# An encoder layer on one core: the mixer's key block ahead of its values, and the values as 2x2 blocks with seven products in three pairs

## The chip, the core and the metric

One Trainium2 chip, of which the kernel uses one core. The metric is the device time of one execution in microseconds (us). A core has TensorE for matrix products (PE in the profile, its weight loads PEld), VectorE (DVE), ScalarE (ACT), GpSimd (POOL) and the queues that issue transfers, SyncE's (SP) above all.

## The reference

One layer on 256 tokens of 2048 values in float32: a gated feed-forward network, a mixer, and a second feed-forward network, each with a norm in front and behind.

```python
ff = swiglu(rms_norm(x, pre_norm_ffn1[layer]), w_ffn1_gate_up[layer], w_ffn1_down[layer])
x = x + 0.5 * rms_norm(ff, post_norm_ffn1[layer])
h = rms_norm(x, pre_norm_mix[layer])
q_h, i_h, f_fwd, f_bwd, g_h, q_a, k_a, v_a = jnp.split(h @ w_mix_in[layer], split_at, axis=-1)
y_h = hgrn2_mixer(q_h, i_h, f_fwd, f_bwd, g_h, ...)
y_a = window_attention(q_a, k_a, v_a, ...)
mixed = jnp.concatenate([y_h, y_a], axis=-1) @ w_mix_out[layer]
x = x + rms_norm(mixed, post_norm_mix[layer])
...
```

The change is in `h @ w_mix_in`, a product of 256x2048 with 2048x6656. Its columns 1024 to 2047 are `i_h`, the **values** of the recurrence; columns 6144 to 6655 are keys and values of the attention, called the **key block** here. The other columns are projected in pairs of heads later.

## The kernel before, in words

**Precision.** Every operand of a large product is taken apart into a high part of reduced precision (a cast on ScalarE, L177) and the low rest (a subtraction on VectorE, L178). A product is then three matmuls: high by high, high by low, low by high. A weight tile of 128x2048 (`raw`, three buffers, 1 MB) is taken apart in two halves of 128x1024, named `h` and `l`, with five buffers each. The tokens lie transposed in `xt`, as high and low parts of 16 chunks of 128 input values; in a chunk stand 256 tokens, two halves `m` of 128.

**The norm.** `xt` holds the tokens times the gain, without the norm's factor. The factor of each token (`rs2`) comes from the squares of the residual X (`square_x`, L255, on ScalarE, one quarter of 512 values at a time), a sum and a scale on VectorE (L183, L185), a power on GpSimd (L187) and a copy (L264). It is applied to the products afterwards: where tokens lie along partitions by a scale of ScalarE, where they lie along columns by the matrix `R`. `spread` (L284) makes `R`: two multiplications of a unit matrix, a matmul by ones (L291) and a copy out of the accumulators (L292).

**Four blocks with seven products.** Class `Blocks` computes a 256x1024 result as 2x2 blocks, input values two chunks (a *pair*, 256 values) at a time. A plain pair takes 8 block products of 3 matmuls (24), a mixed pair seven (21), at the price of sums of the token blocks (`sums_of`, L406) and of the weight blocks (`seven`, L476, with the additions L486, L490 and L492 on VectorE), and of a `fold` at the end (L526) that adds four product banks into the four sums. There are eight accumulator banks in all, four named `pa` and four `pb`. Sums of token blocks of very different size would lose precision; so the second half of the tokens is first multiplied by a power of two, the **ratio** of the two halves' factors (`even`, L1073), and the norm's factor is replaced by `rest` (`power_and_rest`, L266). Before the change the two feed-forward networks and the output projection use these blocks, and the mixer's input projection uses none.

**The start of the mixer.** The stage before (`finish`, L736) ends with a list whose order on TensorE, VectorE and ScalarE is that of the source (`manual_schedule`, L828): updates of X, transposes of X into `xt` (L211, L228, L233), and between them the products of chunks 0 to 7 with the first 512 value columns (`LeadN`, L345), in two banks named `vbanks`. Behind it nothing has a fixed order, and the scheduler sets it by when it takes things to be ready:

```python
for cg in range(2):
    sl = [pa(), pa()] if cg else vbanks
    if cg == 0:
        pre_stats()
        ...
    proj_N(w_in, 1024 + cg * 512, 512, xt, sl, k0=0 if cg else 8)
    for m in range(2):
        nc.scalar.mul(vh[:, m, cg * 512 : (cg + 1) * 512], sl[m], rs2[:, m : m + 1])
```

The matmuls of `proj_N` are L375 to L377 (`products_N`). Then comes the key block, also by `proj_N_pieces` with `spread()` at its piece 16, and then four head pairs by `headpair` (L1597; matmuls L322 and L327).

Of the kernel before, what the change touches and what calls it, by code (L numbers as in the profile page):

```python
# [11 lines left out]
F32 = mybir.dt.float32  # L12
F32R = mybir.dt.float32r
# [24 lines left out]
def hymba_layer_kernel(  # L38
# [37 lines left out]
    def nm(s):  # L76
        uid[0] += 1
        return f"{s}_{uid[0]}"

    def pa():  # L80
        return psum.tile([P, 512], F32, tag="pa", name=nm("pa"))
# [94 lines left out]
    def split_act(hi, lo, src):  # L176
        nc.scalar.copy(hi, src)  # L177
        nc.vector.tensor_tensor(lo, src, hi.bitcast(F32), ALU.subtract)  # L178
# [62 lines left out]
    def pre_stats():  # L241
        with tc.issue_after(last["act"].ins):
            pre_stats_now()
# [37 lines left out]
        nc.vector.tensor_scalar(rest[:, 1:2], rest[:, 1:2], two[:, 0:1], None, ALU.mult)  # L281
        nc.vector.tensor_copy(rest[:, 0:1], rs2[:, 0:1])

    def spread(factor=rs2, n=2):  # L284

        ps = pb()
        for m in range(n):
            nc.vector.tensor_scalar(
                R[:, m * P : (m + 1) * P], ident, factor[:, m : m + 1], None, ALU.mult
            )  # L290
        nc.tensor.matmul(ps[:, : n * P], ones, R[:, : n * P], start=True, stop=True)  # L291
        nc.vector.tensor_copy(R[:, : n * P], ps[:, : n * P])  # L292


    def xcol(xt, k, part=None):
# [83 lines left out]
    def proj_N(*a, **kw):  # L379
        for _ in proj_N_pieces(*a, **kw):  # L380
            pass

    def proj_N_pieces(w, c0, n, xt, slot, k0=0):

        kn = 2048 // n
        half = kn // 2
        for kc in range(k0 // kn, KT // kn):
            hs, ls = split_load(source_N(w, c0, n, kc))
            for m in range(2):
                for kk in range(kn):  # L390
                    i = kk // half
                    products_N(xt, slot, m, kc * kn + kk, hs[i], ls[i], kk % half * n, n)
                    yield
# [215 lines left out]
    class Pairs(Blocks):  # L609
# [26 lines left out]
        def source(self, u):  # L636
            return Pairs.part(self.w, u, self.now)
# [267 lines left out]
    def pair_of(xt, u):  # L905
        return xt[u // 4][:, u % 4 * 2 : u % 4 * 2 + 2]

    class Gated(Blocks):


# [127 lines left out]
    def ffn(gated, w_dn, post_gain, again, gain=None, lead=None, aside=None):  # L1038

        with ExitStack() as st:  # L1040
# [31 lines left out]

            def even(u):  # L1073

                x = gated.tiles[u].rearrange("p k i t -> p (k i) t")[:, :, P:T]
                nc.vector.tensor_tensor(
                    x, x.bitcast(F32), R[:, None, 0:P].to_broadcast([P, 4, P]), ALU.mult
                )

            def sums_in(u):  # L1080
                x = gated.tiles[u].bitcast(F32)
# [428 lines left out]
    def again_from(src):  # L1510
# [4 lines left out]

        return again

    vbanks = [pa(), pa()]
    xt = ffn(
        gated,  # L1520
        w_ffn1_down[0],
        post_norm_ffn1,
        again_from(x[0]),
        gain=lambda: later["cols"][:, 0:16],
        lead=LeadN(w_mix_in[0], 1024, vbanks),
        aside=other_vectors,
    )
    cols = later["cols"]
# [3 lines left out]
    with ExitStack() as s2:  # L1532
# [21 lines left out]
        def lower_bounds():  # L1554
            l0, l1 = cols[:, 32:48], cols[:, 48:64]
            nc.vector.tensor_tensor(lbm, l0, l1, ALU.max)
            nc.vector.tensor_tensor(e0, l0, lbm, ALU.subtract)
            nc.vector.tensor_tensor(e1, l1, lbm, ALU.subtract)
            nc.scalar.activation(e0, e0, AF.Exp)
            nc.scalar.activation(e1, e1, AF.Exp)  # L1560
            nc.vector.tensor_tensor(e1, e0, e1, ALU.add)
            nc.vector.reciprocal(e1, e1)
            nc.vector.tensor_tensor(lb, e0, e1, ALU.mult)
            nc.vector.tensor_scalar(oml, lb, -1.0, 1.0, ALU.mult, ALU.add)

        w_in = w_mix_in[0]
        vh = mid.tile([P, 2, 1024], F32, tag="vh", name="vh")
        for cg in range(2):
            sl = [pa(), pa()] if cg else vbanks
            if cg == 0:  # L1570
                pre_stats()
                with tc.issue_after(last["rs2"].ins):
                    lower_bounds()
            proj_N(w_in, 1024 + cg * 512, 512, xt, sl, k0=0 if cg else 8)
            for m in range(2):
                nc.scalar.mul(
                    vh[:, m, cg * 512 : (cg + 1) * 512], sl[m], rs2[:, m : m + 1]
                )

# [34 lines left out]
            return z  # L1616


        sl = [pa(), pa()]
        for i, _ in enumerate(proj_N_pieces(w_in, 6144, 512, xt, sl)):  # L1620
            if i == 16:
                spread()
        va = mid.tile([P, 2, 256], F32, tag="va", name="va")
        kz = mid.tile([P, 2, 256], F32, tag="q", name="kz")
        for m in range(2):
            nc.scalar.mul(kz[:, m, :], sl[m][:, :256], rs2[:, m : m + 1])
            nc.scalar.mul(va[:, m, :], sl[m][:, 256:], rs2[:, m : m + 1])
        kT = mid.tile([P, 2, T], F32, tag="kT", name="kT")

        def turned_keys():  # L1630
# [129 lines left out]
        def gates(half):  # L1760

            sl = [pa(), pa()]
            for _ in proj_N_pieces(w_in, 4096 + half * 512, 512, xt, sl):
                side_step()
            g = mid.tile([P, 2, 512], F32, tag="g", name=nm("g"))
            for m in range(2):
                by = rs2[:, m : m + 1]
                nc.scalar.activation(g[:, m, :], sl[m], AF.Sigmoid, scale=by)
                nc.vector.scalar_tensor_tensor(g[:, m, :], sl[m], by, g[:, m, :], ALU.mult, ALU.mult)
            return g  # L1770
# [246 lines left out]
```

## Time and profile before

| what | value |
|---|---|
| time, median of 3 runs | 1823.05 us (1822.35 to 1823.59) |
| the profiled execution | 1824.3 us |
| its span, first to last instruction | 1822.5 us |
| mean granted clock of TensorE | 0.999 |
| busy: PE, DVE, ACT | 99%, 88%, 62% of the span |

The profile is one execution. A row of a timeline gives start and duration in us, engine, line, operation, output and inputs, shapes and a count; in square brackets stands the idle time of that engine before it and what ended it. A row of a group gives the count, the busy time and the mean duration of one in ns. A window row gives its length, each engine's busy time with a count, the granted clock of TensorE, the share of the transfer engines and GB/s. The chain of waits followed back from the end gives the start and length of each piece.

### The profile page before, as it was taken

To read this page: it belongs to the slowest core of one execution; us is meant where nothing else is said; L and a number is where in the kernel's file an instruction comes from. 1 tells how busy PE (TensorE), PEld (TensorE's weight loads), DVE (VectorE), ACT (ScalarE), POOL (GpSimd) and SP (SyncE) were. 2 spreads that over 40 slices of the span, in tenths; PEclk is the share of its full clock that TensorE was granted. 3 is DMA by queue.
4 is the path that set the end of the run, shared out by engine and by line. 5 is a ranking of instruction groups with operands and counts; after the bars stand their busy time and mean duration, and the time that the engine had idled before them with its cause. 6 is when DMAs were issued, how large, how long until landed. Compare 5 with 4: busy or idle time off the path is not lost.

```text
span 1822.5 us, 23466 instructions
## 1 busy us (share of the span) xinstructions
PE 1808.9 (99%) x8420; PEld 1502.0 (82%) x8420; DVE 1605.0 (88%) x2073; ACT 1137.1 (62%) x1508; POOL 162.9 (9%) x155
## 2 busy tenths in 40 slices
PE   9999999999999999999999999999999999999998
PEld 7888888888888888888888888888888888888886
DVE  7999999999989989477687798899999999998986
ACT  7565666666666657476587556556666666566653
POOL 1011111111011100000000000111111111011110
PEclk9999999999999999999999999999999999999999
DMA  8889999998698995655454456889999999699894
GB/s 303 240 235 284 278 281 257 250 261 247 224 343 263 300 300 191 196 183 176 162 174 150 162 208 243 253 242 266 283 271 269 256 248 252 195 339 302 274 303 160
DMA packets 212052, 447.59 MB, mean 246 GB/s; under 512 B 11752, under 2 KB 46656, under 8 KB 211168
## 3 DMA queue, kind: packets, MB, share of 16 engines
q1 hardware_dynamic: 180032, 385.14, 60.7%
q0 software_dynamic: 31904, 60.96, 19.5%
q8 instruction: 66, 1.08, 0.2%
q14 instruction: 50, 0.41, 0.1%
HBM read 433.46 MB, written 12.60 MB: 245 GB/s over the span
## 4 chain that ended last, share of the span: by engine, by line
PE 86%; DVE 7%; ACT 3%; DMA 2%; issue 2%; POOL 0%; DVEq 0%; ACTq 0%; SPq 0%; POOLq 0%
PE pa L454 37%; PE pb L454 32%; PE pa L322 5%; DVE l L178 4%; PE pa L327 3%; PE pa L377 2%; PE pa L375 2%; PE pa L376 2%; DMA raw<-in_w_ffn_down_dram 2%; ACT h L177 1%; PE pa L1131 1%; PE pb L1131 1%; DMA raw<-in_w_ffn_gate_up_dram 0%; DVE la L178 0%; PE pb L1738 0%
## 5 line engine op out<-in xcount | busy, mean ns | idle before, releaser
L177 ACT CAST h<-raw 128x1024 fp32r<-128x1024 f32 (+1 forms) x867 | 854.8, 1013 | 465.3 <-PE pb L454 152.9
L178 DVE TENSOR_TENSOR l<-raw,h 128x1024 fp32r<-128x1024 f32 (+1 forms) x867 | 987.8, 1170 | 134.4 <-ACT h L177 100.6
L454 PE MATMUL pa<-h,xt 128*128 128x512 f32 x1096 | 384.9, 392 | 0.1
L454 PE MATMUL pb<-h,xt 128*128 128x512 f32 x940 | 336.7, 392 | 0.3 <-DVE pb L1188 0.3
L454 PEld LDWEIGHTS pa<-h,xt 128*128 128x128 f32 x1096 | 206.0, 188 | 44.2 <-DVE xt L233 0.6
L454 PE MATMUL pa<-l,xt 128*128 128x512 f32 x548 | 214.0, 391 | 0.0
L454 PEld LDWEIGHTS pb<-h,xt 128*128 128x128 f32 x940 | 176.5, 188 | 42.5 <-DVE pb L1195 3.6
L454 PE MATMUL pb<-l,xt 128*128 128x512 f32 x470 | 183.3, 390 | 0.0
L967 POOL DMA_DIRECT2D raw<-in_w_ffn_gate_up_dram x78 | 94.6, 1212 | 733.8 <-DVE l L178 665.8
L454 PE MATMUL pb<-h,ht 128*128 128x512 f32 x452 | 159.2, 389 | 0.0
L454 PE MATMUL pa<-h,ht 128*128 128x512 f32 x452 | 159.1, 389 | 0.0
L322 PE MATMUL pa<-xt,h 128*128 128x512 f32 x512 | 124.5, 393 | 0.2 <-ACT h L177 0.2
L454 PEld LDWEIGHTS pa<-l,xt 128*128 128x128 f32 x548 | 103.2, 188 | 20.6 <-DVE l L178 0.8
L454 PE MATMUL pa<-h,xs 128*128 128x512 f32 x312 | 111.6, 389 | 0.0
L322 PEld LDWEIGHTS pa<-xt,h 128*128 128x128 f32 x512 | 93.8, 188 | 18.7 <-ACT h L177 0.6
L454 PE MATMUL pb<-h,xs 128*128 128x512 f32 x312 | 108.7, 389 | 0.0
L454 PEld LDWEIGHTS pb<-l,xt 128*128 128x128 f32 x470 | 88.3, 188 | 16.8
L454 PEld LDWEIGHTS pb<-h,ht 128*128 128x128 f32 x452 | 84.8, 188 | 17.6
L454 PEld LDWEIGHTS pa<-h,ht 128*128 128x128 f32 x452 | 84.9, 188 | 17.5
L454 PE MATMUL pa<-l,ht 128*128 128x512 f32 x226 | 88.2, 390 | 0.9 <-DVE l L178 0.9
L454 PE MATMUL pb<-l,ht 128*128 128x512 f32 x226 | 87.9, 389 | 0.0
L1273 POOL DMA_DIRECT2D raw<-in_w_ffn_down_dram x38 | 46.0, 1212 | 374.2 <-DVE la L178 337.2
(292 smaller groups left out, 2575.6 us busy)
## 6 DMA issues: line engine op xcount, KB each, us to landing
raw<-in_w_ffn_gate_up_dram SPq DMA_DIRECT2D x350, 512.0 KB, 5.9
raw<-in_w_ffn_down_dram SPq DMA_DIRECT2D x88, 1024.0 KB, 7.8
raw<-in_w_mix_in_dram SPq DMA_DIRECT2D x52, 1024.0 KB, 5.0
raw<-in_w_ffn_gate_up_dram POOLq DMA_DIRECT2D x78, 512.0 KB, 8.1
raw<-in_w_ffn_down_dram POOLq DMA_DIRECT2D x38, 512.0 KB, 10.1
raw<-in_w_mix_out_dram SPq DMA_DIRECT2D x16, 1024.0 KB, 5.0
ht<-away SPq DMA_DIRECT2D x24, 512.0 KB, 10.3
away<-ht SPq DMA_DIRECT2D x16, 512.0 KB, 7.0
```

Source lines behind the costliest of these rows:

```text
L177: nc.scalar.copy(hi, src)
L178: nc.vector.tensor_tensor(lo, src, hi.bitcast(F32), ALU.subtract)
L322: nc.tensor.matmul(slot[f], weights(hs, kk, f), xcol(xt, k), start=(k == 0), stop=(k == KT - 1))
L327: nc.tensor.matmul(slot[f][:, 0:T], weights(ls, kk, f), xcol(xt, kh * 8 + kk, 0), start=False, stop=False,)
L375: nc.tensor.matmul(dst, xh, h[:, o : o + n], start=(k == 0), stop=False)
L376: nc.tensor.matmul(dst, xh, l[:, o : o + n], start=False, stop=False)
L377: nc.tensor.matmul(dst, xl, h[:, o : o + n], start=False, stop=(k == KT - 1))
L454: nc.tensor.matmul(self.bank(at), lhs, rhs, start=(n == 1), stop=n in (ends, self.of[at]), skip_group_check=n > ends,)
L967: nc.gpsimd.dma_start(raw[:, 0:1024].rearrange("p (k c) -> p k c", k=2), self.source(u, g)[:, :, 1], accum_op=ALU.add,)
L1131: nc.tensor.transpose(bank[:, o : o + P], zs[m][:, k * P : (k + 1) * P], ident)
L1273: nc.gpsimd.dma_start(raws[i][:, 0:1024].rearrange("p (k c) -> p k c", k=2), Pairs.part(w_dn, u, r)[:, :, 512:1024], accum_op=ALU.add,)
```

## The change

The stage before now leads in chunks 0 to 7 of the key block in place of the first value columns. The whole rest of the key block and of the values stands in a block whose order on TensorE, VectorE and ScalarE is that of the source. In it the squares of the last quarters, the power and the ratio come first, around the key block's products; then the second half of the tokens is multiplied by the ratio, pair by pair, as soon as the key block has read it. The values are then one set of 2x2 blocks over 1024 columns, in the order of pairs 0 to 7, with pairs 3, 5 and 6 mixed. Since the tokens now carry the ratio, `R` and the gates use `rest` in place of `rs2`. The diff:

```diff
--- before.py
+++ after.py
@@ -281,7 +281,7 @@
         nc.vector.tensor_scalar(rest[:, 1:2], rest[:, 1:2], two[:, 0:1], None, ALU.mult)
         nc.vector.tensor_copy(rest[:, 0:1], rs2[:, 0:1])
 
-    def spread(factor=rs2, n=2):
+    def spread_begin(factor, n=2):
 
         ps = pb()
         for m in range(n):
@@ -289,7 +289,11 @@
                 R[:, m * P : (m + 1) * P], ident, factor[:, m : m + 1], None, ALU.mult
             )
         nc.tensor.matmul(ps[:, : n * P], ones, R[:, : n * P], start=True, stop=True)
-        nc.vector.tensor_copy(R[:, : n * P], ps[:, : n * P])
+        return ps[:, : n * P]
+
+    def spread(factor=rs2, n=2):
+
+        nc.vector.tensor_copy(R[:, : n * P], spread_begin(factor, n))
 
 
     def xcol(xt, k, part=None):
@@ -905,6 +909,13 @@
     def pair_of(xt, u):
         return xt[u // 4][:, u % 4 * 2 : u % 4 * 2 + 2]
 
+    def even_half(x):
+
+        x = x.rearrange("p k i t -> p (k i) t")[:, :, P:T]
+        nc.vector.tensor_tensor(
+            x, x.bitcast(F32), R[:, None, 0:P].to_broadcast([P, 4, P]), ALU.mult
+        )
+
     class Gated(Blocks):
 
 
@@ -1072,10 +1083,7 @@
 
             def even(u):
 
-                x = gated.tiles[u].rearrange("p k i t -> p (k i) t")[:, :, P:T]
-                nc.vector.tensor_tensor(
-                    x, x.bitcast(F32), R[:, None, 0:P].to_broadcast([P, 4, P]), ALU.mult
-                )
+                even_half(gated.tiles[u])
 
             def sums_in(u):
                 x = gated.tiles[u].bitcast(F32)
@@ -1515,14 +1523,14 @@
 
         return again
 
-    vbanks = [pa(), pa()]
+    kvbanks = [pa(), pa()]
     xt = ffn(
         gated,
         w_ffn1_down[0],
         post_norm_ffn1,
         again_from(x[0]),
         gain=lambda: later["cols"][:, 0:16],
-        lead=LeadN(w_mix_in[0], 1024, vbanks),
+        lead=LeadN(w_mix_in[0], 6144, kvbanks),
         aside=other_vectors,
     )
     cols = later["cols"]
@@ -1565,17 +1573,97 @@
 
         w_in = w_mix_in[0]
         vh = mid.tile([P, 2, 1024], F32, tag="vh", name="vh")
-        for cg in range(2):
-            sl = [pa(), pa()] if cg else vbanks
-            if cg == 0:
-                pre_stats()
-                with tc.issue_after(last["rs2"].ins):
-                    lower_bounds()
-            proj_N(w_in, 1024 + cg * 512, 512, xt, sl, k0=0 if cg else 8)
+
+        class Values(Blocks):
+
+
+            def source(self, u):
+                return Pairs.part(w_in, u, 1)
+
+            def left_sums(self, u):
+                return self.sums[u]
+
+            def folded(self):
+                return [
+                    [y[:, n, :] for n in range(2)]
+                    for y in (
+                        keepy.tile([P, 2, 512], F32, tag=f"yt{4 + m}", name=nm("y"), bufs=1)
+                        for m in range(2)
+                    )
+                ]
+
+        def value_sums(u):
+
+            z, s = (keepy.tile([P, 4, P], F32, tag=f"sy{i}", name=nm("vs"), bufs=1) for i in range(2))
+            x = pair_of(xt, u).bitcast(F32)
+            whole = z.rearrange("p j t -> p (j t)").rearrange("p (k t) -> p k t", k=2)
+            nc.vector.tensor_tensor(whole, x[:, :, 0, :], x[:, :, 1, :], ALU.add)
+            w = keepy.tile([P, 4, 2, P], F32R, tag=f"yt{VALUES.index(u)}", name=nm("xs"), bufs=1)
+            split_act(w[:, :, 0, :], w[:, :, 1, :], sums_of(whole, s))
+            values.sums[u] = w
+
+        VALUES = (3, 5, 6)
+        values = Values({u: pair_of(xt, u) for u in range(KT // 2)}, dict.fromkeys(VALUES))
+        va = mid.tile([P, 2, 256], F32, tag="va", name="va")
+        kz = mid.tile([P, 2, 256], F32, tag="q", name="kz")
+        ordered = {mybir.EngineType.PE, mybir.EngineType.DVE, mybir.EngineType.Activation}
+        with tc.manual_schedule(engines=ordered):
+            late = [load(source_N(w_in, 6144, 512, kc)) for kc in (2, 3)]
+            parts = [split(late[0]), ([], [])]
+
+            def next_half(i):
+                for part, of in zip(parts[1], split_half(late[1], i)):
+                    part.append(of)
+
+            def kv(kc, m):
+                hs, ls = parts[kc - 2]
+                for kk in range(4):
+                    products_N(
+                        xt, kvbanks, m, kc * 4 + kk, hs[kk // 2], ls[kk // 2], kk % 2 * 512, 512
+                    )
+
+            square_x(0, 2)
+            square_x(0, 3)
+            next_half(0)
+            square_x(1, 2)
+            square_x(1, 3)
+            next_half(1)
+            pre_stats_now()
+            power_and_rest()
+            kv(2, 0)
+            spread(ratio, 1)
+            for u in range(4):
+                even_half(pair_of(xt, u))
+            values.begin(range(KT // 2))
+            first = split(load(values.source(0)))
+            kv(2, 1)
+            even_half(pair_of(xt, 4))
+            even_half(pair_of(xt, 5))
+            kv(3, 0)
+            value_sums(VALUES[0])
+            kv(3, 1)
+            even_half(pair_of(xt, 6))
+            even_half(pair_of(xt, 7))
             for m in range(2):
-                nc.scalar.mul(
-                    vh[:, m, cg * 512 : (cg + 1) * 512], sl[m], rs2[:, m : m + 1]
-                )
+                nc.scalar.mul(kz[:, m, :], kvbanks[m][:, :256], rs2[:, m : m + 1])
+                nc.scalar.mul(va[:, m, :], kvbanks[m][:, 256:], rs2[:, m : m + 1])
+            values.play(0, *first)
+            values.pos = 1
+            bank = spread_begin(rest)
+            values.work(3)
+            spread_all = nc.vector.tensor_copy(R, bank)
+            values.work(4)
+            value_sums(VALUES[1])
+            values.work(6)
+            value_sums(VALUES[2])
+            values.work(KT // 2)
+            for m in range(2):
+                for n in range(2):
+                    nc.scalar.mul(
+                        vh[:, m, n * 512 : (n + 1) * 512], values.c[m][n], rest[:, m : m + 1]
+                    )
+        with tc.issue_after(spread_all.ins):
+            lower_bounds()
 
 
 
@@ -1616,15 +1704,6 @@
             return z
 
 
-        sl = [pa(), pa()]
-        for i, _ in enumerate(proj_N_pieces(w_in, 6144, 512, xt, sl)):
-            if i == 16:
-                spread()
-        va = mid.tile([P, 2, 256], F32, tag="va", name="va")
-        kz = mid.tile([P, 2, 256], F32, tag="q", name="kz")
-        for m in range(2):
-            nc.scalar.mul(kz[:, m, :], sl[m][:, :256], rs2[:, m : m + 1])
-            nc.scalar.mul(va[:, m, :], sl[m][:, 256:], rs2[:, m : m + 1])
         kT = mid.tile([P, 2, T], F32, tag="kT", name="kT")
 
         def turned_keys():
@@ -1764,7 +1843,7 @@
                 side_step()
             g = mid.tile([P, 2, 512], F32, tag="g", name=nm("g"))
             for m in range(2):
-                by = rs2[:, m : m + 1]
+                by = rest[:, m : m + 1]
                 nc.scalar.activation(g[:, m, :], sl[m], AF.Sigmoid, scale=by)
                 nc.vector.scalar_tensor_tensor(g[:, m, :], sl[m], by, g[:, m, :], ALU.mult, ALU.mult)
             return g
```

## The prediction

> **What bounds the kernel now.** I read the page first, for the shares of the engines, then the busy time by windows around the start of the mixer, then the chain that ended last in order of time, and at the end the timelines of ScalarE and VectorE.
>
> ```profile
> PE 1808.9 (99%) x8420; PEld 1502.0 (82%) x8420; DVE 1605.0 (88%) x2073; ACT 1137.1 (62%) x1508; POOL 162.9 (9%) x155
> ```
>
> ```profile
> 718.60:729.50 10.90, 10.90 (x50) 8.98 (x49) 9.41 (x26) 9.73 (x21) 1.10 (x2) 1.00 0.87 281
> 729.50:751.30 21.80, 21.80 (x98) 18.06 (x97) 10.48 (x12) 10.64 (x11) 0.00 (x0) 1.00 0.65 207
> 751.30:773.50 22.20, 22.20 (x100) 18.39 (x99) 10.12 (x10) 9.85 (x11) 0.00 (x0) 1.00 0.57 190
> ```
>
> ```profile
> 692.67 5.45 PE pa L454 x24
> ...
> 718.63 0.23 PE pa L375
> ...
> 762.88 0.43 PE pb L291 x2
> ...
> 773.53 3.63 PE pa L322 x16
> ```
>
> The window rows give length, then busy time of TensorE, its weight loads, VectorE and ScalarE. TensorE is busy for every microsecond of the three windows; VectorE is at 9.4 of 10.9 in the first and under half later. The stretch that the change rewrites runs from 718.63, where the last transpose of the stage before is done, to 773.53, where the first head pair begins: 54.9 us without a hole. A 512-column product costs 5.45/24 = 0.227 us there. So the kernel has **nothing to lose but TensorE time**: a product less saves 0.227 us, and any wait that the new order gives TensorE is added whole.
>
> **The change part by part.** *Removed products.* Left in the old stretch are 48 products of the first value half (the other 48 were led in earlier), 96 of the second and 96 of the key block: 240. After it 48 are left of the key block, five pairs of the values take 24 and three take 21: 231. Nine fewer are 9 x 0.227 = 2.04 us. The spread of two factors (0.43 us, the row of L291) stays as that of the rest; the one of the ratio is new, a smaller one, at most 0.43. Net of TensorE's work: -1.6 us, so the head pairs would start at 771.9. Loads stay at ten of 1 MB, and a buffer is asked for 10 us or more before its use, against this landing time, so I cost the queue on SP at nothing; if one came late its lateness would be added:
>
> ```profile
> raw<-in_w_mix_in_dram SPq DMA_DIRECT2D x52, 1024.0 KB, 5.0
> ```
>
> *The wait before the ratio's matmul.* In the new order TensorE's queue holds 12 products of chunk 2, first half of the tokens, then the matmul that spreads the ratio, then everything else. The 12 end at 718.63 + 2.72 = 721.35. That matmul needs the ratio, which needs the squares of all eight quarters. ScalarE before:
>
> ```profile
> 698.80 1.99 ACT L177 CAST h<-raw 128x1024 fp32r<-128x1024 f32 x2
> ...
> 712.31 0.65 ACT L255 ACTIVATE jk<-X 128x512 bf16<-128x512 f32 x1
> ...
> 712.92 1.06 ACT L177 CAST h<-raw 128x1024 fp32r<-128x1024 f32 x1
> 713.87 0.65 ACT L255 ACTIVATE jk<-X 128x512 bf16<-128x512 f32 x1
> ...
> 714.49 1.15 ACT L228 ACTIVATE xt<-pa,cols 128x128 fp32r<-128x128 f32 x4
> 715.49 1.18 ACT L228 ACTIVATE xt<-pb,cols 128x128 fp32r<-128x128 f32 x4
> 716.49 1.11 ACT L177 CAST h<-raw 128x1024 fp32r<-128x1024 f32 x1
> 717.43 1.22 ACT L228 ACTIVATE xt<-pa,cols 128x128 fp32r<-128x128 f32 x4
> 718.44 1.15 ACT L177 CAST h<-raw 128x1024 fp32r<-128x1024 f32 x1
> 719.38 1.26 ACT L228 ACTIVATE xt<-pb,cols 128x128 fp32r<-128x128 f32 x4
> 720.39 0.76 ACT L255 ACTIVATE jk<-X 128x512 bf16<-128x512 f32 x1
> ```
>
> Starts lie 0.61 apart behind a square, 0.95 behind a cast, 1.0 behind four scalings (L228), with no hole. The scalings, of the ordered stage before, come in its source order, and casts of later code are set between; I take it that the new ordered stretch is woven in like that. From 712.92 ScalarE then owes three casts (the fourth is the second of the two at 698.80), five squares (the one at 713.87 and the four of quarters 2 and 3) and four groups of scalings: 2.85 + 3.05 + 4.0 = 9.9 us, to 722.8, whatever the weave; the last cast is behind the last square in the new source. VectorE must subtract that cast (1.15) before it may reduce, as the source has it: 724.0. What follows, read where the next stage does the same:
>
> ```profile
> 1143.08 0.15 DVE L185 TENSOR_SCALAR v<-tot 128x1 f32<-128x1 f32 x1
> 1143.96 0.15 DVE L264 COPY scales<-r 128x1 f32<-128x1 f32 x1 [0.73 <-POOL r L187]
> 1144.15 0.24 DVE L269 TENSOR_SCALAR scales<-scales 128x2 int32<-128x2 int32 x2
> ...
> 1145.43 0.15 DVE L272 TENSOR_SCALAR scales<-scales 128x1 int32<-128x1 int32 x1
> ...
> 1145.86 0.29 DVE L288 TENSOR_SCALAR R<-ident,scales 128x128 f32<-128x128 f32 x1
> ```
>
> From scale to copied root 1.03 us by way of GpSimd, with the reduce in front 1.1, twice, since the halves stand one behind the other: 2.2. Then 0.19 to the power's first instruction, 0.24 for two of them, 0.72 from L272 to the end of L288: 1.15. The ratio is spread out at 724.0 + 2.2 + 1.15 = 727.35, and TensorE, idle since 721.35, goes on at about 727.4: **6.1 us lost**. In the old order these instructions ran beside the second value half, which needed none of them; that cover is gone, and behind the waiting matmul stands all of TensorE's queue.
>
> *The queue of VectorE.* It next owes, in source order: the copy of R, eight rescalings of token halves, the low parts of five plain pairs, three sets of sums, three mixed pairs. Durations:
>
> ```profile
> L178 DVE TENSOR_TENSOR la<-raw,ha 128x512 fp32r<-128x512 f32 x25 | 17.1, 683 | 0.0
> ...
> L486 DVE TENSOR_TENSOR raw<-raw 128x1024 f32<-128x1024 f32 x4 | 4.9, 1219 | 0.0
> ...
> L408 DVE TENSOR_TENSOR s<-z 128x256 f32<-128x256 f32 x4 | 1.7, 422 | 0.1
> ...
> L411 DVE TENSOR_TENSOR s<-s,z 128x128 f32<-128x128 f32 x4 | 1.2, 288 | 0.1
> ```
>
> ```profile
> 1104.31 5.75 DVE L178 TENSOR_TENSOR l<-raw,h 128x1024 fp32r<-128x1024 f32 x5
> ...
> 1153.11 0.29 DVE L292 COPY R<-pb 128x128 f32<-128x128 f32 x1
> 1153.43 2.50 DVE L1076 TENSOR_TENSOR xt<-xt,R 128x512 fp32r<-128x512 f32 x4
> ```
>
> In a row they follow each other 0.07 sooner than they last: 1.15 for 1024 columns (5.75/5), 0.61 for 512 (the L1076 row), 0.35 for 256, 0.22 for 128. R: 0.3 + two factors and a copy 0.85. Rescalings: 8 x 0.61 = 4.9. Low parts of pairs 0, 1, 2, 4: 8 x 1.15 = 9.2. Sums, 0.61 + 0.35 + 2 x 0.22 + 0.61 = 2.0 each: 6.0. A mixed pair, first block 0.61, wide addition 1.15, two of 0.61, three low parts 3.45, is 6.4: 19.3. Half of pair 7: 1.15. Together 41.7 us. To it come waits of a queue in source order: a low part waits for its cast, and that cast for the addition just before it on VectorE. The trace of before shows such a turn:
>
> ```profile
> 1054.16 0.68 DVE L492 TENSOR_TENSOR raw<-raw 128x512 f32<-128x512 f32 x1
> ```
>
> ```profile
> 1054.93 1.05 ACT L177 CAST h<-raw 128x1024 fp32r<-128x1024 f32 x1 [1.00 <-DVE raw L492]
> ```
>
> 0.09 from the addition's end to the cast, and 1.05 for it: 1.15, five times (twice a mixed pair, once hidden by pair 7's half), and 0.7 at each of three sets of sums, 7.9 us in all. Between nothing (later code put into the holes doesn't help either, since it isn't what TensorE waits for, but the turns might overlap) and 7.9 I take 7.9: the row shows the turn whole. From 728.1, when the matmul's result is there, VectorE thus hands over the last part of pair 6 at 728.1 + 41.7 + 7.9 = 777.7. TensorE still owes its 6 products and pair 7's 24: 6.8. It ends at **784.6, 11.1 us after 773.53**. Its own work and the first wait alone would end at 778.0; the other 6.6 us are waits at pairs 5 and 6, where two mixed pairs stand next to each other: VectorE needs 2.7 + 8.7 us for a pair with its sums, TensorE 4.76. All eight accumulator banks are held then (four of sums, four of products), so no head pair can fill those holes. The eight additions of the fold (8 x 0.61) lie beside pair 7.
>
> *The clock.* An idle TensorE has a price of its own in this trace:
>
> ```profile
> 1813.16 0.39 PE L454 MATMUL pb<-h,ht 128*128 128x512 f32 x1
> ```
>
> ```profile
> 1817.00:1818.00 1.00, 0.00 (x0) 0.00 (x0) 0.52 (x1) 0.00 (x0) 0.51 (x1) 0.98 0.93 350
> 1818.00:1819.00 1.00, 0.00 (x0) 0.00 (x0) 0.00 (x0) 0.00 (x0) 0.00 (x0) 0.50 1.10 322
> ```
>
> The granted clock (third figure from the right) falls to 0.50 some 4.4 us behind the last product, inside a wait of 6.1. How long it stays there once TensorE works again no row of before shows. Bounds: nothing, and what the start suggests, where transposes take nearly twice their later time until about 8.5 us:
>
> ```profile
> 1.38 2.31 PE L130 MATMUL pb<-idle 128*128 128x512 bf16 x5 [1.38 <-DVE idle L124]
> ...
> 7.47 1.06 PE L211 MATMUL pb<-ident,X 128*128 128x128 f32 x4
> ...
> 14.77 0.60 PE L211 MATMUL pb<-ident,X 128*128 128x128 f32 x4
> ```
>
> First work is at 1.38, so up to 7.1 us at half speed, 3.6 lost. VectorE's queue swallows part of a loss here, as it only meets TensorE again at the rescalings of pairs 6 and 7. I take +1.2. [...]
>
> *Sum.* 11.1 + 1.2 = +12.3 us, made against the profiled execution (1824.3 us, span 1822.5). That lies 1.25 above the median of 1823.05; I move the sum to the median: **1835.4 us**, +0.67%.
>
> **The rivals.** *Only the first wait* (0.18): VectorE gets ahead in pairs 0 to 2, whose products take 5.44 us for its 2.3, and its turns overlap. For it: VectorE is idle half of the old stretch. Against: it starts 6 us late as well. -1.6 + 6.1 + 1.2 = +5.7, 1828.8. *No wait, on the other side* (0.08): the ratio is spread by 721.35. It decides at that point: the last cast and its subtraction would have to leave the chain and the squares to come 6 us sooner, ahead of the scalings at 714.49 to 720.4. Then -1.6 us, 1821.4, and VectorE too starts early enough. Against it: a ScalarE without a hole from 712.3. *The clock stays low* (0.11): as at the start, or it falls again in the waits at pairs 5 and 6 (2 to 3 us each, so under 4.4): another 2 to 5 us, 1838 to 1841. *The order isn't what it says* (0.03): the scheduler takes the spread or the products out of turn; near 1821, or lower if VectorE's relief helps the head pairs.
>
> **How the numbers follow.** The forecast holds 0.60, with 1832 to 1838.5 as its own range: 7.9 us of turns may be 5, the clock 0 to 3.6. The range of 1827.5 to 1840.5 takes in the first rival and most of the third, leaving out the two near 1821. Within 0.2% (3.6 us, about what a measurement of this kernel can tell from no change) lie the two near 1821 but for a sliver, and the edge of the first rival: same 0.11, faster 0.02, slower 0.87.
>
> **What would show it.** TensorE idle from about 721.4 to 727.4, released by VectorE's R (the spread's instruction), and the granted clock at 0.5 just after; then no hole until the fifth value pair; holes of 1 to 3 us released by VectorE's low parts (L178) at pairs 5 and 6; the first head pair near 785 to 787. It is wrong if TensorE stays busy through 721 to 728 (then the chain to the ratio was shorter), or if pairs 5 and 6 have no holes (then VectorE ran ahead), or if the head pairs lose or win time behind it.

## The result, and the profile after

The changed kernel takes **1835.93 us** (median of 5 runs, 1834.75 to 1836.71); the kernel before, beside it, took 1822.68 us (1821.79 to 1823.59). The ratio is 1.0071, 95% interval 1.006 to 1.0083: slower, by 13.25 us. The profiled execution took 1836.34 us with a span of 1834.5 us, 12.0 more than before's span. Line numbers behind L290 have moved: the products of the key block are now L379 to L381, those of the blocks L458, the head pairs' L326, the copy of the ratio's `R` L296, the rescalings L915, the token sums L1600, L412, L415 and L416, the weight additions L490, L494 and L496.

The page's first part and then the windows over the stretch, with the columns known from before:

```profile
PE 1811.0 (99%) x8413; PEld 1502.1 (82%) x8413; DVE 1634.0 (89%) x2127; ACT 1142.1 (62%) x1518; POOL 162.9 (9%) x155
```

```profile
716.00:729.00 13.00, 6.75 (x33) 5.36 (x32) 8.89 (x34) 8.23 (x23) 1.09 (x2) 0.84 0.69 201
729.00:751.00 22.00, 22.00 (x93) 18.07 (x92) 19.72 (x34) 11.36 (x16) 0.00 (x0) 0.94 0.41 145
751.00:774.00 23.00, 21.01 (x88) 16.13 (x86) 18.68 (x25) 9.57 (x12) 0.00 (x0) 0.97 0.41 137
774.00:787.00 13.00, 12.26 (x44) 9.95 (x45) 12.92 (x16) 8.19 (x10) 0.00 (x0) 0.79 0.51 158
```

TensorE has seven instructions fewer in the whole span and is still busy 2.1 us longer. The windows show both halves of the reason: it stands still for 6.25 us of the first, some 2 of the third and 0.7 of the last, and in between its granted clock is not at 1.00. VectorE, under half busy from 729.5 us on before, is at 19.7 of 22 us.

The chain followed back from the first head pair, in order of time:

```profile
722.38 0.94 ACT h L177
...
723.35 1.23 DVE l L178
...
727.53 0.20 DVE R L288
...
727.78 0.80 PE pb L291 x2
728.58 0.43 PE pa L379
...
755.04 2.05 PE pa L458 x9
...
773.55 1.15 DVE l L178
...
774.74 3.78 PE pa L458 x8
778.52 2.57 PE pb L458 x9
...
786.54 1.59 PE pa L326 x7
```

It runs over ScalarE's last cast and VectorE's chain to the ratio until 727.78, over TensorE until 757, over VectorE's queue, with some of ScalarE's casts for it, from there to 774.7, and over TensorE again. The head pairs begin at 786.54, against 773.53 before: 13.0 us later. One us of them came back further on, since the span grew by 12.0; where, I did not follow.

TensorE's timeline, with the idle time before an instruction and what ended it in brackets:

```profile
721.13 0.39 PE L381 MATMUL pa<-h,xt 128*128 128x512 f32 x1
727.78 0.80 PE L291 MATMUL pb<-R,ones 128*128 128x128 f32 x2 [6.25 <-DVE R L288]
...
769.70 0.39 PE L458 MATMUL pb<-h,xt 128*128 128x512 f32 x1
771.54 0.50 PE L458 MATMUL pa<-h,xt 128*128 128x512 f32 x1 [1.46 <-ACT h L177]
772.35 0.57 PE L458 MATMUL pa<-l,xt 128*128 128x512 f32 x1 [0.30 <-DVE l L178]
...
774.74 0.79 PE L458 MATMUL pa<-l,xt 128*128 128x512 f32 x1 [0.97 <-DVE l L178]
```

These four holes are all of more than 0.1 us between the stage before and the head pairs: one in front of the ratio's matmul, three at pair 6, none at pair 5. The granted clock is the third figure from the right in the windows of 1 us:

```profile
724.00:725.00 1.00, 0.00 (x0) 0.00 (x0) 0.79 (x3) 0.26 (x1) 0.10 (x1) 0.93 0.00 0
725.00:726.00 1.00, 0.00 (x0) 0.00 (x0) 0.37 (x3) 0.00 (x0) 0.48 (x2) 0.50 0.49 53
...
731.00:732.00 1.00, 1.00 (x5) 0.81 (x4) 1.00 (x2) 0.83 (x1) 0.00 (x0) 0.66 0.00 0
...
772.00:773.00 1.00, 0.70 (x3) 0.57 (x3) 0.96 (x2) 0.44 (x1) 0.00 (x0) 0.82 1.02 338
...
779.00:780.00 1.00, 1.00 (x4) 0.76 (x4) 1.00 (x2) 1.00 (x3) 0.00 (x0) 0.77 0.00 0
```

The windows on either side show 1.00 and 0.50; taking these as the only two speeds, 0.93 is 0.86 of a microsecond at full speed and the rest at half: the clock fell at 724.86. In the same way it came back at 731.68, fell again at 772.64 and came back at 779.46. At half speed a 512-column product takes 0.43 us (the chain's row at 728.58) in place of 0.23.

VectorE's timeline gives its queue's two ends and two of its waits:

```profile
728.61 0.29 DVE L296 COPY R<-pb 128x128 f32<-128x128 f32 x1 [0.89 <-PE pb L291]
...
748.01 1.22 DVE L178 TENSOR_TENSOR l<-raw,h 128x1024 fp32r<-128x1024 f32 x1 [0.89 <-ACT h L177]
...
757.42 0.69 DVE L178 TENSOR_TENSOR xs<-vs,xs 128x512 fp32r<-128x512 f32 x1 [0.69 <-ACT xs L177]
...
777.07 3.63 DVE L178 TENSOR_TENSOR l<-raw,h 128x1024 fp32r<-128x1024 f32 x3
```

Of the last three low parts the first and third are pair 7's and the second is the last of pair 6: it is done at about 779.4, 50.8 us after the copy of `R` began. VectorE is busy for 44.1 of these by the window over just that time.

### The profile page after: what moved, and what is told of

Same layout as the page of the kernel before. It is cut to its first block, busy times and chain, and to the rows that moved or that the text cites. A ratio compares the mean times of both kernels' runs of the same rounds, so it can differ in the third digit from the quotient of the medians.

```text
span 1834.5 us, 23523 instructions
## 1 busy us (share of the span) xinstructions
PE 1811.0 (99%) x8413; PEld 1502.1 (82%) x8413; DVE 1634.0 (89%) x2127; ACT 1142.1 (62%) x1518; POOL 162.9 (9%) x155
## 4 chain that ended last, share of the span: by engine, by line
PE 89%; DVE 5%; ACT 3%; DMA 2%; issue 1%; POOL 0%; SPq 0%; DVEq 0%; ACTq 0%; POOLq 0%
PE pa L458 40%; PE pb L458 35%; PE pa L326 5%; DVE l L178 3%; PE pa L331 3%; PE pa L381 1%; PE pa L379 1%; DMA raw<-in_w_ffn_gate_up_dram 1%; PE pa L380 1%; ACT h L177 1%; DMA raw<-in_w_ffn_down_dram 1%; PE pa L1139 1%; PE pb L1139 0%; PE pb L1817 0%; PE pb L1791 0%
## 5 line engine op out<-in xcount | busy, mean ns | idle before, releaser
L458 PE MATMUL pa<-h,xt 128*128 128x512 f32 x1148 | 403.5, 393 | 1.6 <-ACT h L177 1.5
L458 PE MATMUL pb<-h,xt 128*128 128x512 f32 x986 | 352.9, 392 | 0.3 <-DVE pb L1196 0.3
L458 PEld LDWEIGHTS pa<-h,xt 128*128 128x128 f32 x1148 | 215.8, 188 | 47.9 <-ACT h L177 1.9
L458 PE MATMUL pa<-l,xt 128*128 128x512 f32 x574 | 224.6, 391 | 1.7 <-DVE l L178 1.7
L458 PEld LDWEIGHTS pb<-h,xt 128*128 128x128 f32 x986 | 185.1, 188 | 44.3 <-DVE pb L1203 3.7
L458 PE MATMUL pb<-l,xt 128*128 128x512 f32 x493 | 192.2, 390 | 0.0
L458 PE MATMUL pb<-h,ht 128*128 128x512 f32 x452 | 159.2, 389 | 0.0
L458 PE MATMUL pa<-h,ht 128*128 128x512 f32 x452 | 159.1, 389 | 0.0
L458 PEld LDWEIGHTS pa<-l,xt 128*128 128x128 f32 x574 | 108.0, 188 | 24.6 <-DVE l L178 3.8
L326 PE MATMUL pa<-xt,h 128*128 128x512 f32 x512 | 124.5, 393 | 0.2 <-ACT h L177 0.2
L458 PE MATMUL pa<-h,xs 128*128 128x512 f32 x324 | 116.7, 392 | 0.0
L458 PE MATMUL pb<-h,xs 128*128 128x512 f32 x324 | 113.3, 390 | 0.0
L326 PEld LDWEIGHTS pa<-xt,h 128*128 128x128 f32 x512 | 93.8, 188 | 18.6 <-ACT h L177 0.6
L458 PEld LDWEIGHTS pb<-l,xt 128*128 128x128 f32 x493 | 92.6, 188 | 17.6
L458 PEld LDWEIGHTS pb<-h,ht 128*128 128x128 f32 x452 | 84.9, 188 | 17.6
L458 PEld LDWEIGHTS pa<-h,ht 128*128 128x128 f32 x452 | 84.9, 188 | 17.5
L458 PE MATMUL pa<-l,ht 128*128 128x512 f32 x226 | 88.0, 390 | 0.1
L458 PE MATMUL pb<-l,ht 128*128 128x512 f32 x226 | 87.9, 389 | 0.0
```

Source lines behind the costliest of these rows:

```text
L326: nc.tensor.matmul(slot[f], weights(hs, kk, f), xcol(xt, k), start=(k == 0), stop=(k == KT - 1))
L458: nc.tensor.matmul(self.bank(at), lhs, rhs, start=(n == 1), stop=n in (ends, self.of[at]), skip_group_check=n > ends,)
```

## The experiments

Theory **A** is the prediction's: from the ratio on, VectorE's queue in source order sets the end, so that what TensorE loses ahead of pair 6 is partly swallowed. Rival **B**: TensorE has no slack, and each hole and each slow stretch of it is added whole, wherever it is. Smaller rivals are named where they are tried: **C**, the seven products bring their 2.0 us; **D**, it is the two mixed pairs next to each other that cost; **E**, the few buffers of high and low parts do; **F**, VectorE's added work does, in whatever order; **G**, TensorE's fixed order is what ties the other engines. Differences below are of medians, to the kernel before in the same set of runs (1822.03, 1822.87 or 1823.15 us). The traces allow a check that leaves out what varies ahead of the change: from the last row of transposes (L211) to the first product of a head pair is 55.3 us in the kernel before (718.03 to 773.37) and 68.2 in the changed one (718.15 to 786.37), and in every version below this stretch grows by what the medians say, within 1 us.

**No mixed pairs.** All eight pairs take eight products; the sums and the fold are gone, the order stays.

```diff
-        VALUES = (3, 5, 6)
+        VALUES = ()
...
-            value_sums(VALUES[0])
...
-            values.work(4)
-            value_sums(VALUES[1])
-            values.work(6)
-            value_sums(VALUES[2])
```

> The changed kernel with no mixed pair: all eight pairs of the values take 24 products, no sums, no fold. Theory A (from the ratio on, VectorE's queue in source order sets the end, and at pair 6 TensorE waits for it): that queue shrinks by some 25 us, TensorE sets the end again. Its sum is 240 products as before the change (+0.4 us for the ratio's spread), the first wait of 6.3 us and some 2 us of low clock: +8.7 over before, so about 1831.4, 4.5 below the changed kernel, with no hole at pair 6. Rival C (seven products bring what they save, the loss is all in the first wait): nine products more, 2.0 us slower than the changed kernel, about 1838.

Measured: 1831.3 us (1830.5 to 1832.49), ratio 1.0051 (1.0038 to 1.0063), +9.3 us. In its timeline only the first hole is left:

```profile
726.73 0.80 PE L291 MATMUL pb<-R,ones 128*128 128x128 f32 x2 [6.31 <-DVE R L288]
```

So C falls: the mixed pairs, which take nine products off TensorE, make this order about 4 us slower (13.25 against 9.3). And the other 9.3 us are there without them.

**The ratio behind the key block.** The ratio's matmul goes behind all 48 products left of the key block, with the eight rescalings in a row after it; the low parts of the first value pair go ahead of the copy of `R`.

```diff
             kv(2, 0)
-            spread(ratio, 1)
-            for u in range(4):
-                even_half(pair_of(xt, u))
...
             kv(3, 1)
+            values.begin(range(KT // 2))
+            bank = spread_begin(ratio, 1)
+            first = split(load(values.source(0)))
+            nc.vector.tensor_copy(R[:, :P], bank)
+            for u in range(KT // 2):
+                even_half(pair_of(xt, u))
+            value_sums(VALUES[0])
```

> The changed kernel with the ratio's matmul behind all 48 products of the key block, the first pair's low parts ahead of R's copy, the eight rescalings in one row. TensorE then works through most of the chain to the ratio; the first hole shrinks from 6.3 to about 1.5 us and the clock doesn't fall there. Theory A (VectorE's queue sets the end): R is ready some 1.4 us later than in the changed kernel, two low parts (2.3 us) and small waits leave the queue behind it, so the end moves by only -1 to -2: about 1834.4, and the holes at pair 6 grow. Rival B (holes of TensorE add up): the hole and the slow stretch are gone, -7: about 1829.

Measured: 1835.62 us (1834.6 to 1836.8), ratio 1.0073 (1.0061 to 1.0086), +13.6 us. The hole of 6.25 us is gone and TensorE is busy at full clock from 720 to 736, yet nothing is won:

```profile
739.28 0.70 PE L291 MATMUL pb<-R,ones 128*128 128x256 f32 x2 [3.30 <-DVE R L288]
...
772.01 0.49 PE L458 MATMUL pa<-h,xt 128*128 128x512 f32 x1 [1.48 <-ACT h L177]
```

The ratio's matmul no longer waits. The wait has moved to 739, in front of the spread of `rest` (the matmul 256 columns wide, whose `R` stands behind the rescalings and sums on VectorE), with a slow clock from 740.90 on, and stays at pair 6. B as first put, a gain of what the hole had cost (1829 was its forecast), falls; A's 1834.4 is 1.2 us too low; a hole that VectorE's queue causes can be moved without moving the end.

**TensorE kept busy in the first hole.** Extra matmuls of 128 columns into an unused bank, 14 and then 30, stand ahead of the ratio's; their result is not used.

```diff
             kv(2, 0)
+            warm_bank = pb()
+            for i in range(30):
+                nc.tensor.matmul(warm_bank[:, :P], ones, ident, start=True, stop=True)
             spread(ratio, 1)
```

> The changed kernel with 14 more matmuls of 128x128 by ones, results unused, behind the 12 products of chunk 2, so that TensorE is busy through the wait for the ratio and its clock should not fall there. Theory A: the slow stretch lay beside VectorE's queue, so the time stays within 1 us of the changed kernel: about 1835.9, with the key block ending 2 us earlier and longer holes at pair 6. Rival B (the slow clock adds): 2 us faster, about 1833.9.

> As e3_kept_busy with 30 extra matmuls in place of 14, which lasted only 3.1 us in e3_kept_busy and did not keep the clock up: now TensorE works until the ratio is there. Theory A (the slow stretch after the first hole lay beside VectorE's queue): the granted clock stays at 1.0 through 724 to 732 us and the time stays within 1 us of 1835.9. Rival B: 2 us faster, 1833.9.

With 14: 1834.24 us (1832.05 to 1835.77), ratio 1.0065 (1.0053 to 1.0078), +12.2 us, and inconclusive: they lasted 3.1 us, a hole of 3.18 stayed, and the clock still fell for a time. With 30: 1833.68 us (1833.31 to 1833.74), ratio 1.0059 (1.0047 to 1.0072), +10.8 us. The clock stays at 1.00 where the first hole was (one of its windows is below), and by the medians 2.4 us are won, against 13.25. By the traces it is less: the stretch shrinks from 68.2 to 66.6 us, so by 1.6, and the rest of the difference lies ahead of the change. Half speed had cost 2.0 us there. Theory A had these swallowed; B is nearer.

```profile
724.00:728.00 4.00, 4.00 (x32) 3.74 (x32) 2.44 (x13) 0.00 (x0) 0.55 (x1) 1.00 0.76 261
```

VectorE's timeline says how A has to be mended:

```profile
726.80 0.29 DVE L296 COPY R<-pb 128x128 f32<-128x128 f32 x1 [0.76 <-PE pb L291]
...
744.82 1.22 DVE L178 TENSOR_TENSOR l<-raw,h 128x1024 fp32r<-128x1024 f32 x1
...
773.80 2.50 DVE L178 TENSOR_TENSOR l<-raw,h 128x1024 fp32r<-128x1024 f32 x2
```

From the copy of `R` to the last group of low parts it now takes 47.0 us, where the changed kernel took 48.46 (728.61 to 777.07). The wait of 0.89 at 748.01 is gone. It was for a cast, and ScalarE began that cast at 746.92, released by a product of TensorE; this fits a cast that found all five buffers of high parts held by products that were late behind the slow stretch. VectorE's queue is thus tied back to TensorE, and slow products lengthen it; that it is the buffers was not tested apart.

**The mixed pairs apart.** Pairs 2, 4 and 6 in place of 3, 5 and 6.

```diff
-        VALUES = (3, 5, 6)
+        VALUES = (2, 4, 6)
```

> The changed kernel with pairs 2, 4 and 6 mixed in place of 3, 5 and 6, so that no two mixed pairs stand next to each other. Theory A (the sum of VectorE's queue counts): the queue is as long, the time stays within 1.5 us of 1835.9. Rival D (two mixed pairs in a row are the cause, as the prediction put it): the holes go, 3 to 6 us faster, 1830 to 1833.

Measured: 1836.14 us (1833.45 to 1837.01), ratio 1.0074 (1.006 to 1.0088), +14.1 us. The holes behind the first are spread out, in place of lying all at pair 6, and the time is the same within A's 1.5 us; D falls:

```profile
754.47 0.49 PE L458 MATMUL pa<-l,xt 128*128 128x512 f32 x1 [0.76 <-DVE l L178]
766.80 0.50 PE L458 MATMUL pa<-h,xt 128*128 128x512 f32 x1 [1.89 <-ACT h L177]
768.06 0.50 PE L458 MATMUL pa<-l,xt 128*128 128x512 f32 x1 [0.76 <-DVE l L178]
```

**Token sums on GpSimd.** The additions of the three sets of sums leave VectorE's queue for the idle GpSimd, earlier in the source and into other buffers; the casts of the sums stay.

```diff
-            nc.vector.tensor_tensor(whole, x[:, :, 0, :], x[:, :, 1, :], ALU.add)
+            add = nc.gpsimd.tensor_tensor
+            add(whole, x[:, :, 0, :], x[:, :, 1, :], ALU.add)
...
             for u in range(4):
                 even_half(pair_of(xt, u))
+            value_adds(VALUES[0])
```

> The changed kernel with the four additions of each set of token sums on GpSimd, ahead of use, so that VectorE keeps only the subtraction of the low part. Theory A (VectorE's queue sets the end): the queue loses 1.4 us of additions and a turn of 0.7 us three times, 6.3 us, about what TensorE waited for it at pair 6 (6.2 us with the slow clock there); so 5 to 6.3 us faster, 1829.6 to 1831, unless GpSimd slows VectorE down. Rival E (TensorE waits at pair 6 for buffers or casts, not for the queue's length): within 1 us of 1835.9.

Measured: 1832.53 us (1831.51 to 1832.94), ratio 1.0053 (1.004 to 1.0066), +9.7 us, so 3.6 less than the changed kernel. Three sets of additions are 1.4 us each by VectorE's rows, and three waits for the cast of the sums went as well (the row at 757.42 shows one). Less than A's 5 to 6.3 us was won, and far more than E's 1: neither forecast holds. VectorE was slower while GpSimd worked. The two engines' timelines:

```profile
740.12 6.79 DVE L178 TENSOR_TENSOR l<-raw,h 128x1024 fp32r<-128x1024 f32 x4
```

```profile
740.60 1.32 POOL L1615 TENSOR_TENSOR vs<-vs,vs 128x128 f32<-128x128 f32 x1
741.88 2.26 POOL L1607 TENSOR_TENSOR vs<-xt 128x512 f32<-128x512 f32 x1
```

In the changed kernel the same four subtractions lasted 4.63 us.

**The order left free.** The same instructions and tiles, without the order by the source on any engine.

```diff
-        with tc.manual_schedule(engines=ordered):
+        if True:
             late = [
```

> The changed kernel with the same instructions but no order by the source in this stretch: the scheduler puts what it takes to be ready first. If the order is what makes the first hole (the ratio's matmul stands ahead of 36 products that are ready), the hole goes, and VectorE may take later low parts into the turns of the mixed pairs: 1826 to 1831. If the work of VectorE alone counts (rival F), the time is within 2 us of 1835.9.

Measured: 1824.45 us (1823.3 to 1827.17, 11 runs), ratio 1.0009 (1.0 to 1.0018), +1.6 us, below the 1826 to 1831 expected. TensorE's timeline has a first hole of 0.9 us, and 1.1 at pair 6:

```profile
728.67 0.49 PE L291 MATMUL pb<-R,ones 128*128 128x128 f32 x2 [0.93 <-DVE R L288]
...
764.94 0.50 PE L458 MATMUL pa<-h,xs 128*128 128x512 f32 x1 [0.83 <-ACT h L177]
```

This is the largest effect of all: 11.7 of the 13.25 us hang on the order and not on the work, so F falls, and so does E by itself, for the buffers are the same. Which place in the order costs how much, it does not say, since the whole order is freed at once. VectorE's timeline shows what a free queue does at a mixed pair:

```profile
741.96 1.22 DVE L490 TENSOR_TENSOR raw<-raw 128x1024 f32<-128x1024 f32 x1
743.10 0.68 DVE L1600 TENSOR_TENSOR vs<-xt 128x512 f32<-128x512 f32 x1
743.70 0.68 DVE L494 TENSOR_TENSOR raw<-raw 128x512 f32<-128x512 f32 x1
744.37 1.22 DVE L178 TENSOR_TENSOR l<-raw,h 128x1024 fp32r<-128x1024 f32 x1
745.52 0.68 DVE L496 TENSOR_TENSOR raw<-raw 128x512 f32<-128x512 f32 x1
746.12 0.42 DVE L412 TENSOR_TENSOR vs<-vs 128x256 f32<-128x256 f32 x1
```

Sums of the next mixed pair (L1600, L412) lie between the weight additions of this one, so that a low part's cast is ready when its turn comes; there is no wait in these rows.

**The key block first, in the kernel before.** Its key block is led in and finished ahead of the values; nothing else of the change.

```diff
-        lead=LeadN(w_mix_in[0], 1024, vbanks),
+        lead=LeadN(w_mix_in[0], 6144, vbanks),
...
+        proj_N(w_in, 6144, 512, xt, vbanks, k0=8)
```

> The kernel before with one part of the change: the key block is led in and projected first, the two value halves behind it, all in plain products with no ratio and no order by the source. TensorE has the same 240 products: 1822.5 within 1 us, no hole. If it is slower by more than 2 us, the move of the key block has a cost of its own, which both theories leave out.

Measured: 1822.94 us (1821.96 to 1824.3, 11 runs), ratio 1.0001 (0.9991 to 1.001): the move of the key block by itself costs nothing.

**Free order and pairs apart**, the two edits above together.

> The changed kernel without the order by the source in this stretch, and the mixed pairs at 2, 4 and 6 in place of 3, 5 and 6. Nine products fewer at 0.227 us each are 2.0 us that the order left free could still bring; with the pairs at 3, 5 and 6 it brought 1.6 us more than before (1824.45). Theory A (the queue of VectorE, with its casts and sums, sets the end; with the order free it is only just short enough): the place of the pairs says little, 1823.5 to 1825.5. Rival D (mixed pairs next to each other is what costs): 1821.0 to 1822.5, faster than before.

Measured: 1824.17 us (1822.69 to 1825.54, 11 runs), ratio 1.0005 (0.9997 to 1.0014), +1.0 us, as A has it. No version with mixed pairs beat the kernel before.

**The order on one side only.** First on TensorE alone, then on VectorE and ScalarE alone.

```diff
-        ordered = {mybir.EngineType.PE, mybir.EngineType.DVE, mybir.EngineType.Activation}
+        ordered = {mybir.EngineType.PE}
```

> The order by the source for TensorE alone; VectorE and ScalarE are left free, so that casts of the next weights go ahead of the chain of the ratio and between the additions of the token sums. Theory A (VectorE's queue in source order sets the end): the first hole stays and grows by about one cast, 6.3 to 7.5 us, with its slow clock of about 2 us, and the holes of pair 6 go: 1822.9 - 1.6 + 7 + 2 = 1830.3, so 1829 to 1832. Rival G (TensorE's order is what ties the other two): within 1 us of the changed kernel, 1835 to 1837.

Measured: 1833.82 us (1832.19 to 1834.13), ratio 1.0056 (1.0043 to 1.0068), +10.7 us; between the two forecasts, and neither is right. Its timeline and two of its windows:

```profile
727.39 0.80 PE L291 MATMUL pb<-R,ones 128*128 128x128 f32 x2 [6.11 <-DVE R L288]
775.04 0.50 PE L458 MATMUL pb<-h,xs 128*128 128x512 f32 x1 [1.01 <-ACT h L177]
776.30 0.50 PE L458 MATMUL pb<-l,xs 128*128 128x512 f32 x1 [0.76 <-DVE l L178]
```

```profile
726.00:727.00 1.00, 0.00 (x0) 0.00 (x0) 0.88 (x8) 0.00 (x0) 0.06 (x1) 0.79 1.01 414
...
733.00:734.00 1.00, 1.00 (x5) 0.77 (x5) 1.00 (x3) 0.65 (x1) 0.00 (x0) 0.80 0.00 0
```

Holes at pair 6 stay, 1.8 us, and the slow stretch, 726.58 to 733.40, lies over 6.0 us of work and takes 3.0. With the products saved and the ratio's spread (-1.6), 6.1 + 3.0 + 1.8 - 1.6 = 9.3 us, against 9.8 in the span.

```diff
+        ordered = {mybir.EngineType.DVE, mybir.EngineType.Activation}
```

> The order by the source for VectorE and ScalarE alone; TensorE is left free, so that the ratio's matmul stands behind more of the key block's products and each product with a high part ahead of those that need the low part. Theory A: VectorE's queue begins with the ratio at the same time and is as long as before, less what slow products held it up: 1833 to 1835.5, with the holes of TensorE later and none at 721 us. Rival G (TensorE's order is what ties the other two): 1824 to 1827.

Measured: 1834.2 us (1831.12 to 1835.11), ratio 1.0055 (1.0042 to 1.0069), +11.1 us, as A has it:

```profile
728.64 0.49 PE L291 MATMUL pb<-R,ones 128*128 128x128 f32 x2 [1.33 <-DVE R L288]
740.34 0.70 PE L291 MATMUL pb<-R,ones 128*128 128x256 f32 x2 [2.34 <-DVE R L288]
770.07 0.50 PE L458 MATMUL pa<-h,xt 128*128 128x512 f32 x1 [1.55 <-ACT h L177]
```

Freed, TensorE does more of the key block ahead of the ratio, and meets VectorE's queue at 740 (in front of the spread of `rest`) and at 770 instead. G falls with it. Either order alone costs some 11 us, both 13.25, so the terms don't add. A reading that fits, and that no run takes apart, is that an engine held to the source holds the others through what they hand each other.

## Why the prediction was right, and where it was not

- **TensorE has nothing to lose** and **nine products less are 2.0 us**: the count of instructions fell by the seven that follow from it (nine less, two for the ratio), and all that TensorE lost showed in the time: four holes of 9.0 us, 2.0 and 2.9 at half speed, less 1.6, are 12.3 of the 12.9 us by which the stretch grew. This sum is bookkeeping and says nothing of the cause. The 2.0 us of the products never showed, in any order tried.
- **The first wait, 6.1 us**: 6.25, released by `R`, for the reason given: last cast done at 723.3, ratio on VectorE ready at 727.73 (chain). Shown.
- **VectorE's queue, 41.7 us of work and 7.9 of turns from 728.1, last part of pair 6 at 777.7**: it began 0.5 us later and took 50.8 in place of 49.6 (44.1 busy, 6.7 idle), to 779.4. The turns came a little cheaper than counted; of the 2.4 us more of work, 1.3 are the seven small operations of `lower_bounds`, woven in between and left out of the forecast. After it TensorE needed 7.0 us (forecast 6.8; it took that part up 0.4 us late, at 779.77, still behind slowed products), so the head pairs came at 786.4 by the start of their products, where the forecast's sum without the clock said 784.6.
- **"Waits at pairs 5 and 6, where two mixed pairs stand next to each other"** failed as to the place and the reason. There is no hole at pair 5, and with the pairs apart the time is the same. Which pairs are mixed doesn't decide; the size, 6.6 us, is about what the mixed pairs cost: they made the kernel 4 us slower where their nine products should have made it 2.0 faster.
- **The clock, +1.2 us**: mis-sized, and counted once where it fell twice. At the first hole half speed lay over 3.9 us of work, so 2.0 us lost; keeping TensorE busy there won 1.6 by the traces, 2.4 by the medians. The second fall, at pair 6, stretched its 21 products to 11.0 us (769.9 to 780.9; 4.8 at full speed), 2.7 of the difference being holes; but the last low part came only at 779.4, so most of it lay beside VectorE's queue. The step "VectorE's queue swallows part of a loss" thus holds for the second and for the most part fails for the first. The upper bound of 3.6 us was read from slow transposes at the start; the granted clock reads 1.00 there (windows from 0 to 8 us), so no row confirms it as half speed.
- **The rival "the clock stays low"** argued that holes of 2 to 3 us at pairs 5 and 6 are too short, being under 4.4. They were 1.5, 0.3 and 1.0, and it fell.
- **That the order is what costs** was said only in passing ("waits of a queue in source order"). It was the main thing: 11.7 of 13.25 us.
- **The total**, 1835.4 against 1835.93, is closer than its parts. The queue was 1.7 us late, and the clock's 1.2, which stood beside it in the sum, acted in part through it; the head pairs came 0.6 us later than the two together said, 1.0 us came back behind them, and the medians lie 13.25 us apart where the two profiled spans lie 12.0. Part of the closeness is luck.

Open: why either order by itself already costs about 11 us was read from the traces and not taken apart further; and what keeps the free order from showing the 2.0 us (its holes are 0.9 and 1.1 us, the ratio's matmul 0.4) was not tried.

## What to carry to other kernels

Where one engine is busy for every microsecond, count for each new chain of waits when it ends on the other engines, and what is queued behind it; a gain of 2 us in products is worth nothing if the queue that feeds them grows longer than they are. An order written out by hand made each engine here wait for turns that a free order filled with other work; try the same instructions with the order left free, and on one engine at a time, before blaming the work. And look at the granted clock behind a long hole, which cost more than its length here: the holes of 2.34 to 6.31 us in these traces, and two shorter ones in a row (1.46 and 0.30 at pair 6 of the changed kernel), took the clock to 0.50, and half of what then lay over work was lost (2.0 us behind the hole of 6.25, 3.0 behind that of 6.11), while a hole of 0.9 us with the free order left it at 1.00.

## What the runs showed of the hardware

**The slow clock came in two lengths, and on a grid.** Summed from windows of 1 or 2 us, every stretch at half speed between 716 and 790 us lasted 3.4 or 6.8 us: 6.82 and 6.82 in the changed kernel, 6.82 with the order on TensorE alone, 3.42 and 6.84 with it on VectorE and ScalarE alone, 6.82 and 3.42 with the ratio behind the keys, 3.42 at pair 6 with 30 extra matmuls. What changed was the start: 3.3 us after the last product ended in the changed kernel (721.53 to 724.86), 5.3 with the order on TensorE alone (721.29 to 726.58), inside holes of 6.25 and 6.11 us. Nearly the same hole so cost 2.0 or 3.0 us. Where a trace has two falls, they lie a whole number of 3.41 us, half of the 6.82, apart: 47.78 us, 14 times that, in the changed kernel (724.86 and 772.64); 34.12, 10 times, with the ratio behind the keys (740.90 and 775.02); 44.36, 13 times, with 14 extra matmuls (726.80 and 771.16).

TensorE was not idle ahead of every fall. Cut into slices of 3.41 us along the falls, TensorE's timelines show the clock falling behind slices with 0 to 1.7 us of work (1.65 in 769.23 to 772.64 of the changed kernel) and holding behind those with 1.9 us or more, and behind one with 1.54 (719.75 to 723.17, with the order on TensorE alone). It came back behind slow slices with 3.0 us or more of work and stayed low behind those with 2.7 or less. That is what these traces show; why the clock does so, no run shows.

**GpSimd's additions slowed VectorE.** A subtraction of 1024 columns, 1.15 us in a row, took 1.70 (6.79/4, with the token sums on GpSimd) while GpSimd added. The four subtractions beside some 6 us of additions were stretched by 2.2 us (6.79 against 4.63), not held for the whole of them.
